# Another fixed order of two mixing stages, and another split of the weights' second parts between two engines

## The chip, the cores and the metric

The kernel runs on one core of one Trainium2 chip. The metric is the device time of one execution in microseconds (us), lower is better. The core's engines work side by side, each through its own instructions in the order in which they were issued, and they wait for one another through semaphores: TensorE (PE) for matmuls, VectorE (DVE), ScalarE (ACT), GpSimd (POOL), and SyncE (SP), which here only issues DMAs.

## The reference, cut to what matters

The input x is 512 x 1024 in float32. Two layers follow each other:

```python
h = rms_norm(x, norm_mix_g[l])
proj = h @ w_in[l]                       # 26 groups of 128 columns
o_att  = diff_attention(q, k, v, ...)    # 6 heads: softmax(q0 k0) - lam * softmax(q1 k1)
o_conv = short_conv(b, c, u, conv_w)     # y = b * causal 3-tap conv of c * u
o_rwkv = rwkv7_time_mix(...)             # 6 heads, a recurrence over the 512 positions
x = x + concat(o_att, o_conv, o_rwkv) @ w_out[l]
h = rms_norm(x, norm_mlp_g[l])
x = x + square(relu(h @ w_mlp_up[l])) @ w_mlp_down[l]
```

and at the end a last rms_norm. The part of a layer up to the product with w_out is called the mixing stage here, the rest its MLP stage.

## The kernel before, in words

**Layout.** Everything is kept transposed: x is eight tiles of 128 model channels by 512 positions. A product of 128 output columns is a chain of matmuls over eight channel tiles into one PSUM tile.

**Two-part products.** Each float32 operand is split into a rounded first part (hi) and the rest (lo), and a product takes three matmuls: hi by hi, hi by lo, lo by hi (`passes`, L550 to L559). The weights come in halves of four tiles, 256 KB a DMA, into three `raw` buffers. ACT rounds a half to `whi` (`casts`, L539). The second part `wlo` is raw - whi (`rests`, L548), and a letter of the string LO says for each half of a mixing stage whether DVE (x) or POOL (y) works it out. The first groups of layer 0 (HEAD) always go to DVE. `whi` and `wlo` have three buffers each.

**Order of the products.** PLAN gives, for each layer, the order in which the 26 column groups of w_in are multiplied. Groups 0 to 2, 3 to 5 and 6 to 8 are q, k and v of three pairs of attention heads; 9 to 14 the convolution's; 15 to 17, 18 to 20 and 21 to 23 r, k and v of the three pairs of recurrent heads; 24 and 25 the small inner products. After them come the eight column groups of w_out, in two halves of four channel tiles, and two groups of w_mlp_up. Loads, casts and second parts follow the same order (`halves_`).

**The steps.** A mixing stage is written as some twenty Python generators, each of which issues one instruction (or one group of small matmuls) at each step. Their letters: d loads (SP), w casts (ACT), x and y second parts (DVE, POOL), m the large matmuls (PE), e, q and n the entry and its norm, k constants, g decay rates, h the gate, R, S, T the three pairs of recurrent heads, r, s, t the block inverses that these need, A, B, C the three pairs of attention heads, U, V the convolution, o, p, i, N the output, its squares and the next norm. The two strings in ORDER, one for each layer, spell out in which order the steps are issued: `drive` (L157) reads "m3 R w" as three steps of m, one of R, one of w. Since every engine works through its instructions in the order of issue, this string fixes the order on each engine. Nothing reorders it later; only the waits for data and for free buffers come on top.

**The pieces that matter below.**

- Recurrent heads (`rwkv_pair`, L766): Gram products (pg), copied by ACT into nn; turned blocks; then products with the inverse (pzw, pap, pbs), then six steps of state (pst, L933, and L934 on DVE), then the outputs, a centring product (pc), a head norm and the gate. The head norm sums squares on PE (phs), takes an inverse square root in twelve small DVE operations (`rsqrt_steps`, L248), widens it on ACT (L739) and turns it back on PE (phb).
- Block inverse (`rwkv_inverse`, L985): POOL masks nn (nm, L990), DVE folds it (L992), it goes to DRAM and back in another layout (dn, nb); POOL then runs 30 small operations in 15 dependent pairs (tt L1004, xb L1006); the result goes through DRAM again (dm, xd); DVE spreads it (L1013, L1021) and turns it (yi, L1032); then PE and the copies alternate: px, py, pz, pzz.
- Attention (`att_pair`, L1096): q and k go through DRAM into stacked tiles; then for each of two heads and four query blocks two score products (sc), a masked maximum on DVE (L1163), two exponentials on ACT (L1168), small DVE operations (L1170, L1172), the difference of the two maps (L1174), transposes on PE (ptt) and a copy (L1183); at the end of a head the product with v (po).
- PSUM tiles come from three tags: mm (2 buffers, large products), at (2, attention), rp (4, everything else).

The MLP stages are issued by ordinary loops and have nothing to do with the strings.

Of the kernel before, what the change touches and what calls it, by code (L numbers as in the profile page):

```python
# [21 lines left out]
S = 512  # L22
# [3 lines left out]
C = 64  # L26
# [14 lines left out]
PLAN = ((24, 18, 15, 0, 3, 6, 25, 19, 21, 16, 1, 4, 22, 7, 20, 17, 2, 5, 11, 8, 13, 23, 9, 12, 14, 10),  # L41
        (24, 18, 15, 0, 3, 6, 19, 21, 25, 16, 1, 4, 7, 20, 22, 17, 11, 2, 13, 5, 9, 12, 8, 23, 14, 10))
# [7 lines left out]
LO = ("xxxxyxxxyxxxxxyyxyyxxyxyyxyxxxyxxyyyxyxyxyxxxxyyxxyxyyxyxxyyyxyxyxxxyxxx",  # L50
      "yyxxxxxxyyxxxyyyyyyxxxxyxyyyyyxxxyyyyyxxxyyyxyxxxyxyyyxyyxxxxyxyyxxxxyxy")

ORDER = (
# [1389 lines left out]
```

## Time and profile before

| | |
|---|---|
| median of three runs | 1301.89 us (1301.4 to 1303.5) |
| profiled execution, its own time | 1301.58 us |
| its span, first to last instruction | 1299.8 us |
| mean granted TensorE clock | 0.996 |
| mixing stage of layer 0 ("stage one") | 0 to 312.58 us |
| MLP stage of layer 0 ("stage two") | 312.58 to 648.42 us |
| mixing stage of layer 1 ("stage three") | 648.42 to 949.44 us |
| MLP stage of layer 1 and the last norm ("stage four") | 949.44 us to the end |

The bounds of the stages are read off the chain that ended last: it runs without a break from the second of the two early w_mlp_up groups on (312.58 and 949.44), and at 648.42 the products of w_in begin.

How to read the lines in the next section. The page's first part gives for each engine its busy time, its share of the span and its instructions; the second part gives busy tenths in 40 slices. A row of the table by stages has the stretch, its length, then busy time and count for PE, PEld (weight loads), DVE, ACT and POOL, then the granted clock, the share of the DMA engines and GB/s. A row of the waits says who waited for whom: us in total, times, the longest. A row of the groups has line, engine, operation, output and inputs with their shapes and count, then busy us and the mean ns of one, then the idle time before them and what ended it. A row of a tile's view has min/median/max in ns. A row of the timeline has start, length, line, engine, operation and count, and in brackets the idle time before it and what ended it.

### The profile page before, as it was taken

How to read it: one execution, taken by the hardware profiler on the slowest of the kernel's cores; microseconds unless marked ns; L12 is line 12 of the kernel's file. 1: busy time of each engine (PE TensorE's matmuls, PEld its weight loads, DVE VectorE, ACT ScalarE, POOL GpSimd, SP SyncE). 2: the span in 40 equal slices, each digit the busy share in tenths (PEclk: the TensorE clock that was granted, in tenths of full speed). 3: DMA queues.
4: the chain of work that ended last, by engine and by line, in shares of the span. 5: the costliest groups of instructions: out<-in, count | busy, mean ns of one | idle time of the engine just before them, and what ended most of it. 6: DMA issues, size and time to landing. Idle time of an engine off the chain costs nothing.

```text
span 1299.8 us, 25202 instructions
## 1 busy us (share of the span) xinstructions
PE 1270.7 (98%) x9531; PEld 1068.8 (82%) x9531; DVE 931.6 (72%) x1924; ACT 692.9 (53%) x1431; POOL 350.9 (27%) x440
## 2 busy tenths in 40 slices
PE   9999999999999999999999999999999999999997
PEld 6777777787889989889887777878778898898987
DVE  6777768967866938756557787877698497595754
ACT  6764655555644626436465756455567264363552
POOL 1362526233310201102317344451432021020010
PEclk9999999999999999999999999999999999999998
DMA  6523333132332332330235232331423323323121
GB/s 217 149 64 100 111 94 92 48 123 82 101 126 90 105 106 86 111 98 25 98 112 141 72 118 83 90 102 51 138 74 126 109 93 109 100 90 105 58 81 66
DMA packets 84425, 128.12 MB, mean 99 GB/s; under 512 B 21456, under 2 KB 24912, under 8 KB 84304
## 3 DMA queue, kind: packets, MB, share of 16 engines
q1 hardware_dynamic: 83584, 125.96, 30.9%
q8 instruction: 75, 1.23, 0.4%
q10 hardware_dynamic: 720, 0.55, 0.1%
q14 instruction: 46, 0.38, 0.1%
HBM read 117.30 MB, written 9.18 MB: 97 GB/s over the span
## 4 chain that ended last, share of the span: by engine, by line
PE 77%; DVE 10%; issue 2%; ACT 2%; DMA 1%; POOL 0%; POOLq 0%; SPq 0%; DVEq 0%; ACTq 0%
PE dn L180 23%; PE pj L180 14%; PE pp L180 11%; PE po L180 8%; PE up L180 8%; PE dnF L180 3%; DVE slo_p L1302 3%; DVE s L1307 2%; PE sc L180 1%; PE ptt L185 1%; PE pg L180 1%; DVE u L1324 1%; DVE c L1324 1%; PE pyy L180 1%; PE pst L180 0%
## 5 line engine op out<-in xcount | busy, mean ns | idle before, releaser
L1237 POOL TENSOR_TENSOR ml<-m,mh 128x512 fp32r<-128x512 f32 x64 | 101.6, 1587 | 504.4 <-ACT mh L1236 496.2
L231 ACT CAST whi<-raw 128x512 fp32r<-128x512 f32 x154 | 95.3, 621 | 201.6 <-PE dn L180 182.1
L232 DVE TENSOR_TENSOR wlo<-raw,whi 128x512 fp32r<-128x512 f32 x154 | 119.8, 778 | 85.8 <-ACT whi L231 85.6
L180 PE MATMUL dn<-ml,whi 128*128 128x512 f32 x448 | 174.4, 389 | 0.0
L180 PE MATMUL dn<-mh,whi 128*128 128x512 f32 x448 | 174.4, 389 | 0.0
L180 PE MATMUL dn<-mh,wlo 128*128 128x512 f32 x448 | 174.3, 389 | 0.0
L180 PE MATMUL pj<-ahim,whi 128*128 128x512 f32 x392 | 159.5, 407 | 0.0
L180 PE MATMUL pj<-alom,whi 128*128 128x512 f32 x392 | 159.4, 407 | 0.0
L180 PE MATMUL pj<-ahim,wlo 128*128 128x512 f32 x392 | 158.9, 405 | 0.0
L548 POOL TENSOR_TENSOR wlo<-raw,whi 128x512 fp32r<-128x512 f32 x64 | 87.7, 1371 | 197.4 <-ACT whi L539 165.3
L539 ACT CAST whi<-raw 128x512 fp32r<-128x512 f32 x138 | 85.3, 618 | 98.3 <-PE pj L180 42.5
L180 PE MATMUL pp<-thi,slo_p 128*128 128x256 f32 x352 | 100.1, 284 | 0.2
L180 PE MATMUL pp<-thi,shi_p 128*128 128x256 f32 x352 | 99.7, 283 | 0.5
L180 PE MATMUL pp<-tlo,shi_p 128*128 128x256 f32 x352 | 99.2, 282 | 0.0
L180 PEld LDWEIGHTS dn<-mh,wlo 128*128 128x128 f32 x448 | 84.1, 188 | 17.5
L180 PEld LDWEIGHTS dn<-mh,whi 128*128 128x128 f32 x448 | 84.1, 188 | 17.4
L180 PEld LDWEIGHTS dn<-ml,whi 128*128 128x128 f32 x448 | 84.1, 188 | 17.3
L1370 DVE TENSOR_TENSOR x<-dn,x 128x512 f32<-128x512 f32 x56 | 38.6, 690 | 75.7 <-PE dn L180 75.7
L180 PEld LDWEIGHTS pj<-ahim,whi 128*128 128x128 f32 x392 | 74.0, 189 | 15.1 <-issue 1.2
L180 PEld LDWEIGHTS pj<-ahim,wlo 128*128 128x128 f32 x392 | 74.0, 189 | 14.5 <-issue 1.0
L180 PEld LDWEIGHTS pj<-alom,whi 128*128 128x128 f32 x392 | 74.0, 189 | 14.4 <-issue 1.1
L180 PE MATMUL pp<-bhi,shi_p 128*128 128x256 f32 x264 | 74.7, 283 | 2.0 <-DVE u L1324 2.0
(399 smaller groups left out, 3244.5 us busy)
## 6 DMA issues: line engine op xcount, KB each, us to landing
raw<-wts SPq DMA_DIRECT2D x392, 256.0 KB, 2.7
qs<-dqhi SPq DMA_DIRECT2D x24, 128.0 KB, 3.8
ks<-dkhi SPq DMA_DIRECT2D x24, 128.0 KB, 4.0
x<-xT SPq DMA_DIRECT2D x8, 256.0 KB, 5.1
dqhi<-qhi SPq DMA_DIRECT2D x6, 256.0 KB, 3.4
dqlo<-qlo SPq DMA_DIRECT2D x6, 256.0 KB, 2.4
dkhi<-khi SPq DMA_DIRECT2D x6, 256.0 KB, 2.4
dklo<-klo SPq DMA_DIRECT2D x6, 256.0 KB, 2.8
```

Source lines behind the costliest of these rows:

```text
L180: ins = nc.tensor.matmul(*a, **k)
L185: ins = nc.tensor.transpose(*a, **k)
L231: act.copy(hi[:, :n], raw[:, :n])
L232: (pool if a and lean[0] else dve).tensor_tensor(lo[:, :n], raw[:, :n], hi[:, :n].bitcast(F32), ALU.subtract)
L539: yield act.copy(hi[:, :n], raw[:, :n])
L548: yield eng.tensor_tensor(lo[:, :n], raw[:, :n], hi[:, :n].bitcast(F32), ALU.subtract)
L1237: pool.tensor_tensor(lo, m, hi.bitcast(F32), ALU.subtract)
L1302: dve.tensor_tensor(lo, src, hi.bitcast(F32), ALU.subtract)
L1307: dve.tensor_tensor(t, a, b, op)
L1324: dve.tensor_tensor(out, pt, b, ALU.add)
L1370: dve.tensor_tensor(x[j], pt, x[j], ALU.add)
```

## The change

Only constants change: PLAN, LO and both strings of ORDER. No function is touched. The steps are the same in number and kind (2259 in layer 0, 2208 in layer 1). In layer 0, 33 of the 72 weight halves have their second part on POOL instead of 28, and 39 on DVE instead of 44 (six of them are HEAD's). In layer 1 it is 24 on POOL instead of 36, and 48 on DVE instead of 36.

The order strings are long. Below are PLAN, LO, and of ORDER the lines with the first steps and those in which the inverse of the first pair of layer 0 goes through px, py, pz, pzz (the r's) and on to pzw (an R), then those with the end of the second pair's head norm in layer 1 (S):

```diff
-PLAN = ((24, 18, 15, 0, 3, 6, 25, 19, 21, 16, 1, 4, 22, 7, 20, 17, 2, 5, 11, 8, 13, 23, 9, 12, 14, 10),
-        (24, 18, 15, 0, 3, 6, 19, 21, 25, 16, 1, 4, 7, 20, 22, 17, 11, 2, 13, 5, 9, 12, 8, 23, 14, 10))
+PLAN = ((24, 18, 15, 0, 3, 21, 6, 19, 25, 16, 22, 1, 4, 20, 7, 17, 2, 23, 5, 8, 11, 13, 9, 12, 14, 10),
+        (24, 18, 15, 0, 3, 21, 6, 25, 19, 16, 1, 4, 22, 7, 20, 17, 2, 5, 23, 11, 8, 13, 12, 9, 14, 10))
...
-LO = ("xxxxyxxxyxxxxxyyxyyxxyxyyxyxxxyxxyyyxyxyxyxxxxyyxxyxyyxyxxyyyxyxyxxxyxxx",
-      "yyxxxxxxyyxxxyyyyyyxxxxyxyyyyyxxxyyyyyxxxyyyxyxxxyxyyyxyyxxxxyxyyxxxxyxy")
+LO = ("yyxxxyxyxyxxyyyyxyxyxyyyxyxyxyxyxyxyxyxxxyxyxyyyxxxyxyxxxyyxxxyyyyxyxyxx",
+      "xxyxxxxyxxyyxxxxxxxxxxxyyyyxxxxyxxxxyyxyxxyyyxxxxxxyxxyyxxyyyxyyxyxxxxxx")
...
-         "d g d6 w x e d q m e w m x m w m2 d x m2 e m d m q e d m e d q d m q m d m e m e d m2 d q m q m d m e w m d m w m q d m d m x m d w m2 x d m d "
+         "g d7 w x e d q e m w m x w m x d m e m d m q d e m d e m d q2 m d e2 m d2 q m w d m q e d m x w m d m d m x m d w m2 d q m d m x e m d m2 d "
...
-         "A m r w S A d m S m r m r S x B m2 S d r A m S r m r m2 r m2 w m A m2 B2 m r y B2 A r2 m2 A d A m B r A2 r m r A m A m2 B2 R A w B A m A B "
+         "m h m2 r d m r w m r m S m3 r m y S m r m4 S A m d w A m2 S h m A r m y A2 m A2 m A m A m d S m S m2 r A m S w r2 m r2 m3 S A m h m x m r d "
+         "S2 m r S2 r A m S A m r S2 A r2 m A S A r w m A S m y A m r A m r2 d S m S2 r A m2 r m r m R S A3 m R2 m S m A m w B S A x B m R S d A B3 A "
...
-         "C m C S B T m C m S m S C m S m2 B T m S C m2 w B T m2 T S B y C S C T2 B d m T S m t T m2 S2 B t T S m B t S B S B m2 S m T B w S m T2 B x "
-         "t3 m T m2 T U d m U m2 S2 m T U T m S T m t U m T m T2 S w t U m T m5 S T m3 S t m T S m t y m S m2 w V m S T d m S m4 x m3 S d S t2 m S m t "
+         "m B2 S m B2 m3 S w S B x T d m T B S m S m2 S m S m2 T S m2 T m2 T w B S B S T2 B T S T t m B2 U S y t T B t S B T d B T2 B3 S m B T S m B S "
+         "m T t3 B S m T B S T B S B S B m S B T S m B S m T B S B m T S T B2 S B m2 S T t2 B t S t m B m t m T m w m2 t T m S2 T2 m S m3 T t m T m y "
```

105 rows, old and new, of the table ORDER are left out of this document.

## The prediction

> **What bounds the kernel now.** I read the page's first two parts, then the busy table over the four stages, then the waits of PE, then the timeline at the longest waits.
>
> ```profile
> PE 1270.7 (98%) x9531; PEld 1068.8 (82%) x9531; DVE 931.6 (72%) x1924; ACT 692.9 (53%) x1431; POOL 350.9 (27%) x440
> PE   9999999999999999999999999999999999999997
> ```
> ```profile
> 0.00:312.58 312.58, 301.65 (x2821) 237.32 (x2822) 234.40 (x593) 184.27 (x425) 114.36 (x181) 1.00 0.36 110
> 312.58:648.42 335.84, 334.44 (x1900) 293.76 (x1900) 235.48 (x366) 167.37 (x297) 60.24 (x40) 1.00 0.29 93
> 648.42:949.44 301.02, 294.46 (x2810) 235.89 (x2810) 221.37 (x559) 171.77 (x406) 122.41 (x183) 1.00 0.33 100
> 949.44:1299.80 350.36, 340.18 (x2004) 301.80 (x2002) 240.39 (x406) 169.51 (x304) 53.84 (x36) 0.99 0.29 93
> ```
>
> TensorE bounds it, at the full granted clock (1.00) through both mixing stages (rows one and three). The change reaches only these. PE stands still there for 312.58 - 301.65 = 10.9 us and 301.02 - 294.46 = 6.6 us. That 17.5 us is most of what an order can win; what it can lose has no such end. The other two stages keep their instructions and their times. The next view is what PE waited for, stage one and then stage three.
>
> ```profile
> PE px L180 <- DVE yi L1032: 2.3, 3, 1.0
> PE ptt L185 <- DVE pp L1174: 2.1, 4, 0.7
> ```
> ```profile
> PE phby L185 <- ACT rwy L739: 2.1, 2, 1.7
> PE ptt L185 <- DVE pp L1174: 1.2, 1, 1.2
> PE pst L180 <- DVE st L934: 0.7, 1, 0.7
> ```
>
> So PE waits at the ends of serial chains: the block inverse (px), the softmax (ptt), the head norm (phby), the state (pst). All 864 `m` letters of a stage are large matmuls that fill such chains. I therefore compare, old order with new, how much PE work stands between the two ends of a chain.
>
> **The change, part by part.** Both strings hold the same letters, 2259 and 2208 steps, and PE gets the same steps. Only their order moves, so nothing is saved on PE itself, and each term below is a wait. A large matmul counts 0.233 us, from this row of the chain of work (9.80/42):
>
> ```profile
> 656.05 9.80 PE pj L180 x42
> ```
>
> *1. The inverse chain.* From the first Gram product (pg) of a head pair to px run two copies, a mask, two DRAM round trips, 30 small POOL operations and a transposition. In stage one, pair 0:
>
> ```profile
> 58.76 0.35 ACT L831 COPY nn<-pg 128x256 f32<-128x256 f32 x1
> ```
> ```profile
> 68.39 0.21 POOL L1004 TENSOR_TENSOR tt<-nb,xb 64x15 f32<-64x15 f32 x1 [0.96 <-DMA nb<-dn]
> ```
> ```profile
> 85.17 0.21 POOL L1006 TENSOR_TENSOR xb<-xb,tt 64x15 f32<-64x15 f32 x1
> ```
> ```profile
> 95.51 0.59 PE L180 MATMUL px<-yi,ee 64*64 64x64 f32 x25 [0.96 <-DVE yi L1032]
> ```
>
> The chain took 36.7 us (58.76 to 95.51), 17.0 of them in POOL's small operations. PE, covering it, ran out 0.96 us early. Between pg and px the old order of stage one has 102, 105 and 109 large matmuls for pairs 0, 1 and 2; the new one has 103, 78 and 154. The smaller PE groups beside them, each counted from its first matmul to the next group's (pzz below: 171.35 to 171.98), go from 9.7, 9.7 and 7.3 us to 5.6, 8.4 and 10.4. With 0.233 us a large matmul, cover goes from 33.5, 34.2 and 32.7 us to 29.6, 26.6 and 46.3. Pair 2 gains cover; pair 0 loses 3.9 us and pair 1 loses 7.6. POOL's own load inside the 30 operations moves too: pair 0 gets three weight halves where it had one, pair 1 two where it had three.
>
> ```profile
> L548 DVE TENSOR_TENSOR wlo<-raw,whi x74: 671/683/1627, 24.1 to 938.6; 128x512 fp32r<-128x512 f32 x74
> L548 POOL TENSOR_TENSOR wlo<-raw,whi x64: 1263/1290/1811, 22.9 to 943.3; 128x512 fp32r<-128x512 f32 x64
> ```
> ```profile
> L548 POOL TENSOR_TENSOR wlo<-raw,whi 128x512 fp32r<-128x512 f32 x28 | 38.3, 1367 | 87.6 <-ACT whi L539 66.3 <-DVE st L934 13.1 <-PE po L180 6.0
> ```
>
> That is +2.6 us for pair 0; pair 1 loses 1.29 and one more POOL operation of that size, -2.6. Upper end: the chain keeps its length but for POOL's load, and PE's other waits beside it stay (36.7 - 0.96 - 33.5 = 2.2 us; I use it for both). Pair 0 then waits 36.7 + 2.6 - 29.6 - 2.2 = 7.5 us, pair 1, whose chain I take as long, 36.7 - 2.6 - 26.6 - 2.2 = 5.3 us; less the 2.3 us that go, +10.5 us. Lower end: the chain shrinks with its cover. The last row speaks for some of this: 66.3 us of POOL's idle time before a weight half ended with ACT's whi, so POOL is paced by the weights' turn in the order. Then all px waits vanish, -2.3 us. I take the middle, **+4 us**. In stage three the counts are 104, 100, 114 and 108, 102, 106: no change.
>
> *2. The short links after px.* px, pz and pzz each feed the next PE step through two ACT copies:
>
> ```profile
> 171.35 0.69 PE L180 MATMUL pzz<-x,rt 32*32 32x32 f32 x32
> 171.98 0.44 PE L180 MATMUL sc<-ks,qs 96*128 96x128 f32 x2
> ...
> 173.56 0.34 PE L180 MATMUL pzw<-ab,x 64*64 64x128 f32 x4
> ```
> ```profile
> 172.09 0.75 ACT L1070 COPY x<-pzz 32x256 f32<-32x256 f32 x2 [0.47 <-PE pzz L180]
> ```
>
> The copies end at 172.84, 0.86 us after pzz gave PE free (171.98); with the hand-over some 0.95 us. The old stage one covers all nine links with 1.16 us or more, this one with 1.6. The new one covers px to py with 3 matmuls, 1 and a 0.46 us group, and 3; pzz to pzw with 4, with one 0.8 us group, and 3; one pz link has 0.86. Those below 0.95 lack 0.26, 0.26, 0.26, 0.09, 0.02, 0.15 and 0.25 us, in sum 1.3. The state links run from one pst through DVE to the next:
>
> ```profile
> L180 PE MATMUL pst<-st,ad x60: 217/273/324, 114.1 to 896.8; 128*128 128x64 f32 x60
> L934 DVE SCALAR_TENSOR_TENSOR st<-pst,dc,db x36: 272/280/285, 113.6 to 897.6; 128x64 f32<-128x64 f32 x36
> ```
>
> The need is 0.273 + 0.280 and the hand-overs, some 0.6 us. Five of these 15 links have two matmuls or fewer between (0.47 us) in the new order, none in the old: 0.7 us more. Upper end 2.0, lower end 0 if PE is late anyway: **+1.5 us**. Stage three's balance over the same links is under 0.5 us: nothing.
>
> *3. Softmax links.* From the second score product to the transposes:
>
> ```profile
> L1168 ACT ACTIVATE pp<-pp,mx 128x128 f32<-128x128 f32 (+3 forms) x48 | 26.6, 555 | 13.8 <-DVE mx L1163 13.0 <-DVE rst L263 0.6
> L1163 DVE CUSTOM_DVE_ANT_0 pp<-sc,caus 128x128 f32<-128x128 f32 (+3 forms) x48 | 22.1, 486 | 9.0 <-PE sc L180 8.8
> L1174 DVE SCALAR_TENSOR_TENSOR pp<-pp,sm,pp 128x128 f32<-128x128 f32 (+3 forms) x24 | 15.7, 656 | 0.5
> L1168 ACT ACTIVATION_READ_ACCUMULATOR pp<-pp,mx 128x1 f32 x48 | 9.0, 186 | 0.0
> L1172 DVE SCALAR_TENSOR_TENSOR sm<-s0q,nlam,sm 128x1 f32<-128x1 f32 x24 | 6.4, 268 | 0.4
> L1170 DVE RECIPROCAL sm<-sm 128x1 f32<-128x1 f32 x24 | 3.9, 161 | 13.0 <-ACT pp L1168 12.8
> ```
>
> The need is 0.486 + 0.555 + 0.186 + 0.161 + 0.268 + 0.656 = 2.3 us and queueing. With under 3.3 us of cover stand 9 of 24 links in the old stage one and 12 in the new; 11 and 7 in stage three. At the waits quoted (2.1/9 and 1.2/11 us a link) this is +0.7 - 0.4 = **+0.3 us**; a full softmax need uncovered would be 2.3.
>
> *4. The engine choice.* Stage one takes 5 halves from DVE to POOL (POOL 28 to 33), stage three 12 from POOL to DVE (36 to 24). On DVE those are 12 x 0.683 = 8.2 us more, beside 301.02 - 221.37 = 79.7 us of its idle time; without that cover they would cost the 8.2. What POOL's operations do to DVE is seen here:
>
> ```profile
> 843.34 2.68 DVE L263 SCALAR_TENSOR_TENSOR rst<-rst,rsx 128x8 f32<-128x8 f32 x1
> ```
> ```profile
> 843.48 1.29 POOL L548 TENSOR_TENSOR wlo<-raw,whi 128x512 fp32r<-128x512 f32 x1
> 844.74 1.25 POOL L869 TENSOR_TENSOR pd_2lo<-pd,pd_2hi 128x512 fp32r<-128x512 f32 x1
> ```
> ```profile
> L263 DVE SCALAR_TENSOR_TENSOR rst<-rst,rsx x72: 147/166/2681, 22.0 to 1291.7; 128x8 f32<-128x8 f32 x54, 128x4 f32<-128x4 f32 x12, 128x2 f32<-128x2 f32 x6
> ```
>
> An operation of 0.166 us took 2.68, to the end of two POOL operations, and stage three's 1.7 us wait at phby follows it. Fewer POOL halves in stage three make such hits rarer, but in the new order that same link (second pair, phsy to phby) has 10 matmuls and three transposes where it had 31 and five groups. Two inverse square roots lie interleaved in it, 22 operations of 0.166 us, so its own length, 22 x 0.166 + 0.68 + 0.62 = 5.0 us, meets about 3.4 us of cover. A wait of 1.6 stands where one of 1.7 stood. For the rest -0.5 us, between -2.1 (the other quoted waits of stage three, 1.2 + 0.7, and this 0.2) and +2.3.
>
> The Trainium skill ("SBUF — State Buffer", "Who interferes with whom") says that a VectorE instruction with two SBUF inputs and a GpSimd instruction that reads SBUF exclude each other for a whole instruction; the 2.68 us row agrees. By that rule the 12 halves taken off POOL in stage three free up to 12 x 1.29 = 15.5 us of such locks; the first rival below is this case.
>
> *5. The rest.* The products' order moves the value product of a pair by one group and some DMA issues with it; each raw load still goes out on SP three buffers ahead, in the products' order, and the stacked q and k loads keep their place behind them on that queue. The ends of both stages, from the last output products on, are the same but for single letters. Nothing, between -0.5 and +1.
>
> **Sum.** 4 + 1.5 + 0.3 - 0.5 = +5.3 us on the profiled execution's 1301.58 us, which lies 0.3 us under the median of 1301.89: about **1307 us**.
>
> **The rivals.**
>
> *Faster.* The waits are collisions of DVE with POOL, not short cover. For it: the 2.68 us row, and the lighter POOL in stage three. Against it: stage one gets more POOL halves, and its counted cover shrinks. If POOL's pacing lets the inverse chain shrink (-2.3), the short links cost nothing, and stage three loses its quoted waits at ptt and pst (1.2 + 0.7) with 0.2 at phby, it is -4.4: 1297 us. It decides from where the px chain of pair 1 in stage one runs in under 29 us.
>
> *No change.* The chain shrinks half way and the wins of stage three meet it: +1, 1302.5 us.
>
> *Much slower.* The chain keeps its length: 10.5 + 2.0 + 0.7 us, and no gain in stage three: +13.2, 1315 us. For it: POOL's part was 17.0 us though its 30 operations are small.
>
> **How the numbers follow.** Forecast (1303.5 to 1311) 0.48; much slower 0.20; no change 0.14; faster 0.18. This measurement tells about 0.2% (2.6 us) from no change. Slower 0.48 + 0.20 = 0.68, same 0.14, faster 0.18. The range from 1298 to 1316 leaves out part of the fastest and of the slowest case.
>
> **What would show it.** Stage one longer by 3 to 8 us, most of it as waits of px on yi for pairs 0 and 1 and none for pair 2; stage three within 1.5 us; a phby wait near its middle; DVE busy up in stage three, POOL down by about 15 us. Wrong, if px of pairs 0 and 1 waits under 1 us each: then the chain follows its cover. Also wrong, if stage three moves by over 3 us: then the engine choice is worth more than I gave it.

## The result, and the profile after

The changed kernel takes **1308.03 us** (median of five runs, 1306.51 to 1310.77), the kernel before 1302.44 us beside it (five runs, 1301.4 to 1304.77). The ratio is 1.0045 with a 95% interval of 1.0034 to 1.0055: it is slower by 5.6 us. The profiled execution of after took 1308.03 us itself, 6.45 us more than that of before, so its stages can be set against those of before.

The table by stages of after, with the bounds read off its chain in the same way (columns: stretch, its length, then busy time and count of PE, PEld, DVE, ACT and POOL, the granted clock, DMA share, GB/s):

```profile
0.00:320.76 320.76, 306.54 (x2823) 237.36 (x2824) 228.43 (x588) 184.74 (x426) 116.47 (x186) 1.00 0.34 107
320.76:656.75 335.99, 334.39 (x1899) 293.26 (x1898) 237.28 (x368) 166.75 (x296) 57.53 (x38) 1.00 0.28 93
656.75:955.42 298.67, 295.65 (x2811) 235.91 (x2811) 217.11 (x569) 173.78 (x406) 105.61 (x173) 1.00 0.33 101
955.42:1306.20 350.78, 340.07 (x2003) 301.04 (x2001) 241.58 (x406) 169.67 (x304) 52.98 (x36) 0.99 0.28 92
```

Stage one is longer by 320.76 - 312.58 = **8.2 us**, stage three shorter by 301.02 - 298.67 = **2.35 us**; the stages that kept their code moved by 0.15 and 0.42 us. In stage one PE stands still for 320.76 - 306.54 = 14.2 us (10.9 before), and is booked as busy for 4.9 us more with the same work. The second part is waiting too: a large matmul is booked with 0.39 us, but the next one starts after 0.233 us if nothing holds it, so each break of the stream hides up to 0.16 us in "busy".

What PE waited for in stage one of after (columns: who for whom, us in total, times, the longest):

```profile
PE ptt L184 <- DVE pp L1173: 2.3, 5, 0.8
PE px L179 <- DVE sm L1169: 2.1, 1, 2.1
PE pssm L179 <- DVE accm L335: 1.6, 1, 1.6
...
PE pj L179 <- DVE pk L660: 0.9, 1, 0.9
PE pj L179 <- DVE vf L1130: 0.9, 1, 0.9
PE sc L179 <- ACT pT L1182: 0.8, 3, 0.4
PE prbm L179 <- issue: 0.8, 1, 0.8
PE phby L184 <- ACT rwy L738: 0.8, 1, 0.8
```

px waits once, for 2.1 us, where it waited three times and 2.3 us before (the profile names sm, the DVE operation right behind yi). The new waits are others: pssm, the product of the first norm at the entry, 1.6 us; and large products (pj) that wait for an eviction, twice 0.9 us. In stage three of after the same view has the phby waits (2.1 us) and that of the state (0.7 us) gone:

```profile
PE ptt L184 <- DVE pp L1173: 1.0, 2, 0.6
PE pv L184 <- DVE zv L665: 0.8, 1, 0.8
PE prbf L179 <- DVE rrf L263: 0.6, 1, 0.6
```

To count the hidden part too, I took for every matmul the time to the next one's start, less the time under which the fastest fifth of its shape stay in stage one of before (0.23 us for a large one), and summed it by what the next matmul writes. "Short links" are all PE steps from py to the end of the state, pbv among them. In us, for before, after and two kernels of the experiments below:

| stage one | before | after | s1_order | s1_engines |
|---|---|---|---|---|
| px | 4.2 | 3.5 | 1.5 | 3.0 |
| short links after px, state | 15.3 | 17.8 | 17.8 | 16.3 |
| softmax (sc, ptt) | 10.2 | 12.5 | 13.4 | 10.1 |
| head norms (phs, phb) | 3.8 | 3.1 | 2.6 | 6.3 |
| entry (pssm, prbm, pw) | 2.2 | 4.4 | 3.8 | 2.0 |
| large products (pj, po) | 21.0 | 22.1 | 24.3 | 21.6 |
| Gram products and all others | 15.5 | 16.5 | 17.3 | 15.9 |
| sum | 72.2 | 79.9 | 80.6 | 75.2 |

| stage three | before | s3_order | s3_engines | s3_all |
|---|---|---|---|---|
| px | 1.2 | 1.9 | 1.2 | 1.2 |
| short links, state | 17.2 | 16.4 | 16.7 | 16.1 |
| softmax | 8.6 | 8.7 | 10.4 | 8.4 |
| head norms | 4.5 | 2.4 | 2.6 | 2.4 |
| entry | 0.5 | 0.5 | 0.9 | 0.9 |
| large products | 19.5 | 18.8 | 19.6 | 18.7 |
| Gram products and all others | 16.1 | 19.1 | 15.7 | 17.5 |
| sum | 67.6 | 67.8 | 67.1 | 65.3 |

So the 8 us of stage one are no single wait. They lie in the short links (+2.5), the softmax (+2.3), the entry (+2.2), large products and others (+2.1); px and the head norms fell (0.7 each). One caution: in the profiled execution of s1_order 3.4 us of stage one (22.10 to 25.51) ran at half the granted clock, which puts up to some 2 us into its column; before, after and s1_engines have no such stretch in stage one (the last section).

**My theory after the result** was that the order takes cover from many chains at once, and that px, the largest term of the forecast, was not one of them. The rival was collisions: POOL's operations hold DVE's, and the engine choice decides.

### The profile page after: what moved, and what is told of

Its sections match the earlier page's. It is cut to its first block, busy times and chain, and to the rows that moved or that the text cites. A ratio compares the mean times of both kernels' runs of the same rounds, so it can differ in the third digit from the quotient of the medians.

```text
span 1306.2 us, 25237 instructions
## 1 busy us (share of the span) xinstructions
PE 1276.6 (98%) x9531; PEld 1067.6 (82%) x9531; DVE 924.4 (71%) x1931; ACT 694.9 (53%) x1431; POOL 332.6 (25%) x433
## 4 chain that ended last, share of the span: by engine, by line
PE 80%; DVE 11%; issue 3%; ACT 2%; DMA 2%; POOL 1%; SPq 0%; POOLq 0%; DVEq 0%; ACTq 0%
PE dn L179 23%; PE pj L179 18%; PE pp L179 10%; PE po L179 8%; PE up L179 7%; PE dnF L179 3%; DVE slo_p L1301 3%; DVE s L1306 2%; PE sc L179 1%; PE ptt L184 1%; DMA raw<-wts 1%; DVE c L1323 1%; PE pg L179 1%; DVE u L1323 1%; PE pst L179 1%
## 5 line engine op out<-in xcount | busy, mean ns | idle before, releaser
L547 POOL TENSOR_TENSOR wlo<-raw,whi 128x512 fp32r<-128x512 f32 x57 | 74.9, 1314 | 210.7 <-ACT whi L538 181.1
L179 PEld LDWEIGHTS dn<-ml,whi 128*128 128x128 f32 x448 | 84.1, 188 | 17.2
L179 PEld LDWEIGHTS pj<-ahim,whi 128*128 128x128 f32 x392 | 74.1, 189 | 17.3 <-DVE pk L660 1.4
```

Source lines behind the costliest of these rows:

```text
L179: ins = nc.tensor.matmul(*a, **k)
L547: yield eng.tensor_tensor(lo[:, :n], raw[:, :n], hi[:, :n].bitcast(F32), ALU.subtract)
```

## The experiments

All leave nothing of the computation out. Times are ratios to the kernel before, run beside each on the same chip, with 95% intervals. For lengths of stages I use two marks of each trace: A, from the start to PE's first product with w_mlp_down in layer 0 (360.52 us in before), and B, from the first pj of layer 1 to the same product there (349.18). Where a stage was left as in before, A was 360.52, 360.64, 362.13, 362.42 and 362.60, and B 349.02 to 349.72. So one profile tells 2 us in stage one and 0.7 us in stage three. The last section shows where the 2 us come from: the granted clock. A of after (368.82) is free of it.

### Each stage alone

```diff
 s1_all: PLAN[0], LO[0], ORDER[0] of after; PLAN[1], LO[1], ORDER[1] of before
 s3_all: PLAN[0], LO[0], ORDER[0] of before; PLAN[1], LO[1], ORDER[1] of after
```

> PLAN, LO and order string of layer 0 from after, layer 1 as before: stage one alone is changed. In the one profile of after, stage one is 320.76 us against 312.58 (+8.2), stage three 298.67 against 301.02 (-2.35). If the two stages are independent, this kernel is 8 us over before (about 1310), its stage three 301 us as in before. If part of the 8.2 us is chance of one execution, it is +4 to +6 and another profile shows other waits. In the forecast's terms (+4 for px, +1.5 short links, +0.3 softmax) it would be +5.8.

> PLAN, LO and order string of layer 1 from after, layer 0 as before: stage three alone is changed. If the stages are independent, 2.3 us under before (about 1300). The forecast's terms for this stage (order 0, engine choice -0.5) say within 0.5 us of before.

Measured: s1_all 1.0076 (1.0064 to 1.0089), 9.9 us slower; A 370.56, B 349.72. s3_all 0.9979 (0.9969 to 0.9988), 2.7 us faster; A 362.60, B 346.91, as in after (346.68). The stages are independent, and both effects come again: stage one +8 (A 368.82 in after and 370.56 here, against a mean of 361.7) and stage three -2.6. The waits come again too, within 0.2 us (s1_all: px 2.2 us once, pssm 1.4, pj twice 0.9), so they belong to stage one's new order and engines, not to one execution. The forecast's -0.5 at most for stage three is refuted.

### Order and engine choice of stage three

The order of after with each half on the engine that it had before, and the other way round:

```diff
 s3_order, LO[1] on after's PLAN[1] and ORDER[1]:
-xxyxxxxyxxyyxxxxxxxxxxxyyyyxxxxyxxxxyyxyxxyyyxxxxxxyxxyyxxyyyxyyxyxxxxxx
+yyxxxxxxyyyyxxyyxyyxxxxyyyxyyyxxyyxxxxxyxyyyyyxyxyxyyyxyyxxxxyxyyxxxxyxy
 s3_engines, LO[1] on before's PLAN[1] and ORDER[1]:
-yyxxxxxxyyxxxyyyyyyxxxxyxyyyyyxxxyyyyyxxxyyyxyxxxyxyyyxyyxxxxyxyyxxxxyxy
+xxyxxxxyxxxxxxyyxxxxxxxyyxxxyyxyxyxxyyxxxxyxxxyyxxxyxxyyxxyyyxyyxyxxxxxx
```

> Layer 1 has after's order of products and steps, but each half of the weights keeps the engine that it had before (36 on POOL, 36 on DVE): a letter x or y is changed in its place. If the gain of stage three comes from 12 halves fewer on POOL (fewer DVE operations stretched beside POOL's), this shows none of it: 0 to +2 us against before. If it comes from the order (the head norm's and softmax links have other cover), this shows all of it, -2 us.

> Layer 1 has before's order of products and steps, but each half has the engine that after gives it (24 on POOL, 48 on DVE): a letter x or y is changed in its place. If the gain of stage three comes from fewer collisions, this has it: -2 us or more, with the 1.7 us wait of phby gone. If it comes from the order, 0; if DVE as the longer queue delays the chain ends, +1 to +2.

Measured: s3_order 1.0010 (1.0001 to 1.0019), B 349.46; s3_engines 0.9993 (0.9984 to 1.0002), B 348.61. Neither has the gain (s3_engines has 0.9 us, with none inside its interval), and both together have 2.7 us: the expectation of one cause fails. The table of stage three shows why. Each of the two takes the head norm's waits away (4.5 to 2.4 and 2.6), and each pays it back elsewhere: the order with the old engines in Gram and other products (+3.0, among them 0.6 us of pot), the engines with the old order in the softmax (+1.8; ptt waits 2.8 us). Together the softmax stays at 8.4. An order and the engines beside it are one choice.

The stretch of DVE says the same. Summing, over DVE's operations that ran over 0.3 us above the fast tenth of their form beside a POOL operation, what they ran over: 20.8 us in stage three of before (22 operations), 11.5 in s3_order (12, with the same 36 halves on POOL), 16.3 in s3_engines (19), 10.1 in s3_all (11). So which operations meet counts for more than how many halves POOL has. Nor does this sum give the time: s3_order halves it and gains nothing.

### One letter

```diff
 LO[1]:
-yyxxxxxxyyxxxyyyyyyxxxxyxyyyyyxxxyyyyyxxxyyyxyxxxyxyyyxyyxxxxyxyyxxxxyxy
+yyxxxxxxyyxxxyyyyyyxxxxyxyyyyyxxxyyyyyxxxyyyxxxxxyxyyyxyyxxxxyxyyxxxxyxy
 ORDER[1]:
-S T m3 S t m T S m t y m S m2 w V m S
+S T m3 S t m T S m t x m S m2 w V m S
```

> Before, with one single weight half of stage three (group 8, second half; the one on POOL at 843.48) moved from POOL to DVE. There an operation of 0.166 us on DVE took 2.68 us, to the end of this half and of the next POOL operation, and PE waited 1.7 us at phby behind it. If POOL's operation holds DVE's, this one letter takes away 1.3 us or more of that wait and the kernel is 1 to 2 us faster; if the DVE operation waited for something else, the phby wait stays and nothing is gained.

Measured: 0.9983 (0.9974 to 0.9991), **2.2 us faster**, B 347.43. The timeline of this kernel at the place where an operation took 2.68 us before:

```profile
843.65 0.20 DVE L263 SCALAR_TENSOR_TENSOR rst<-rst,rsx 128x8 f32<-128x8 f32 x1
...
843.88 0.17 DVE L264 SCALAR_TENSOR_TENSOR ry<-rst,ry 128x8 f32<-128x8 f32 x1
843.99 0.69 DVE L548 TENSOR_TENSOR wlo<-raw,whi 128x512 fp32r<-128x512 f32 x1
```

The operation takes 0.20 us again, the half runs on DVE for 0.69 us behind the chain, and of the phby waits (2.1 us) this is left:

```profile
PE phby L185 <- ACT rwy L739: 0.4, 1, 0.4
```

POOL's operation held DVE's, and one letter is worth nearly as much as the whole change of stage three (2.2 and 2.7 us, with intervals that overlap). The rule of the Trainium skill named in the prediction ("SBUF — State Buffer", "Who interferes with whom") says this of a DVE operation with two SBUF inputs; the run agrees with 0.20 us for 2.68.

### Order and engine choice of stage one

```diff
 s1_order, LO[0] on after's PLAN[0] and ORDER[0]:
-yyxxxyxyxyxxyyyyxyxyxyyyxyxyxyxyxyxyxyxxxyxyxyyyxxxyxyxxxyyxxxyyyyxyxyxx
+xxxxxxxxyxxyxxyyxxyxyxxyxyxxyxyxxyxxyyxyxyxyxxyyxxyxyyxyxxyyyxyxyxxxyxxx
 s1_engines, LO[0] on before's PLAN[0] and ORDER[0]:
-xxxxyxxxyxxxxxyyxyyxxyxyyxyxxxyxxyyyxyxyxyxxxxyyxxyxyyxyxxyyyxyxyxxxyxxx
+xxxxxxxyxyyyxyyyxxxyyyxyxyxyxyxyxyxyxyxxxyxyxyyyxxxyxyxxxyyxxxyyyyxyxyxx
```

> Layer 0 has after's order of products and steps, but each weight half keeps the engine of before (28 on POOL instead of 33); layer 1 as before. Forecast: the loss comes from cover that the order takes away, so nearly all of it stays: +7 to +9 us against before in stage one. Rival (collisions, or POOL's halves between the 30 small operations): 5 halves fewer on POOL give back 3 us or more.

> Layer 0 has before's order, but each weight half has the engine that after gives it (33 on POOL); layer 1 as before. Forecast: within 1.5 us of before. Rival (collisions): +2 us or more. In stage three the two parts of the change did not add (order +1.3, engines -0.9, both -2.7); if an order and its engines belong together, both of these kernels are slower than before by more than the forecast allows.

Measured: s1_order 1.0053 (1.0040 to 1.0066), +6.9 us, A 369.51; s1_engines 1.0024 (1.0016 to 1.0033), **+3.1 us**, A 363.76. Here the parts add up (0.53 + 0.24 against 0.76% for s1_all). The order is the larger part, as forecast, and it costs 6.9 us although px does not wait once in s1_order (1.5 in the table, 4.2 before): the forecast's largest term is not where the order loses. The engine choice costs 3 us where the forecast had 0 for stage one. With before's order its loss lies in the head norms (3.8 to 6.3 in the table). The timeline of s1_engines in the second pair's head norm:

```profile
225.87 1.58 POOL L548 TENSOR_TENSOR wlo<-raw,whi 128x512 fp32r<-128x512 f32 x1 [1.22 <-ACT whi L539]
226.23 1.25 DVE L263 SCALAR_TENSOR_TENSOR rst<-rst,rsx 128x8 f32<-128x8 f32 x1
...
227.41 1.26 POOL L1030 TENSOR_TENSOR ee<-nn,cst 128x512 f32<-128x512 f32 x1
227.51 1.19 DVE L264 SCALAR_TENSOR_TENSOR ry<-rst,ry 128x8 f32<-128x8 f32 x1
...
228.74 0.62 ACT L739 COPY rwy<-ry 128x512 f32<-128x512 f32 x1 [2.94 <-DVE ry L264]
```

Two operations of 0.166 us run to the ends of two POOL operations, and PE waits behind them:

```profile
PE phby L185 <- ACT rwy L739: 1.6, 1, 1.6
```

It looks like the collision of stage three once more, made by a half (group 10's second) that the new LO moves from DVE to POOL; no run moves this half back alone. In before only the operation ee met this chain, and PE waited 0.7 us.

After itself does not pay this: with the new order its head norms fell (3.8 to 3.1), and DVE's stretch, summed as above, is 14.9 us in stage one of after, 19.8 in before, 17.9 in s1_order and 25.7 in s1_engines. What the engine choice costs beside the new order (3 us from s1_order to s1_all) is not located, and part of it may be the clock: the mean granted clock is 0.994 in all five runs of s1_all, and 0.995 to 0.997 in those compared of s1_order; the table has 2.0 more at px in after than in s1_order.

### Cover of the inverse chain

In before, for each pair of stage one, 10 large matmuls are put from ahead of px to behind it (px_early10), or 5 from behind to ahead (px_late5); the first pair as an example:

```diff
 px_early10:
-S r m r m A2 r2 m w A m A m2 A m y A m2 B A m r w S
+S r2 A2 r2 w A3 y A B A r m10 w S
 px_late5:
-A m r w S A d m S m r m r S x B m2 S d
+A m6 r w S A d S r2 S x B S d
```

> Before, with the last 10 large matmuls ahead of px put directly behind it, for each of the three pairs of stage one: 2.33 us less cover for each inverse chain, all else in its order. If a chain has a length of its own, as the forecast's upper end took it, px waits 2.3 us longer in each pair: +7 us. If the chain follows its cover (POOL and DVE come to its steps earlier when PE stands), it is under +3.5 us, and the chain from nn to px is shorter by 1 us or more a pair. The forecast's middle lies between, +4.5.

> Before, with the next 5 large matmuls behind px put ahead of it, for each of the three pairs of stage one: 1.17 us more cover for each chain. If a large matmul of cover is worth 0.233 us wherever PE waits, the three px waits (2.3 us) go and the kernel is 2 us faster. If the wait only moves (to py and pz, which lose 5 matmuls of cover and have the two copies between them), it is 0 to +2.

Measured: px_early10 1.0066 (1.0054 to 1.0078), **+8.6 us**; px_late5 0.9989 (0.9981 to 0.9998), -1.4 us. The waits of px in px_early10:

```profile
PE px L180 <- DVE yi L1032: 5.8, 2, 3.2
PE px L180 <- DVE sm L1172: 2.8, 1, 2.8
```

That is 8.6 us for 2.3 in before: 6.3 us for 30 matmuls, 0.21 us each. The chains from nn to px are 36.6, 37.4 and 36.0 us, as long as in before (36.7, 37.3, 36.1). So a chain does **not** follow its cover when only PE's work is moved: the price of the forecast, 0.233 us a matmul, nearly holds. The measured +8.6 is over the +7 for a reason of the hardware, told last. px_late5 takes the three px waits away and gives part of it back: the sum of the head norms rises by 0.9 us (phbk waits 2.0 for 1.2), the short links by 0.8.

Then why did pair 0 wait 2.1 us in after where the forecast's upper end had 7.5, and pair 1 not at all where it had 5.3? From nn to px it took 35.0 and 33.1 us (58.09 to 93.07, 119.81 to 152.90). The rows of the second, from nn to POOL's first operation, the one half that runs among the 30, yi and px:

```profile
119.81 0.37 ACT L830 COPY nn<-pg 128x256 f32<-128x256 f32 x1 [0.79 <-PE pg L179]
```
```profile
129.21 0.21 POOL L1003 TENSOR_TENSOR tt<-nb,xb 64x15 f32<-64x15 f32 x1
```
```profile
138.78 1.29 POOL L547 TENSOR_TENSOR wlo<-raw,whi 128x512 fp32r<-128x512 f32 x1
```
```profile
151.36 0.71 DVE L1031 STREAM_TRANSPOSE yi<-x 128x512 f32<-128x512 f32 x1
```
```profile
152.90 0.29 PE L179 MATMUL px<-yi,ee 64*64 64x64 f32 x4
```

POOL's part, from 129.21 to 142.2, took 13.0 us, where it took 17.7 in before. In both kernels the 30 operations alone take some 12 us (11.6 to 12.2) with their hand-overs. The rest is what the order puts among them: in before 5.4 us of other operations (three halves, a pd_lo) for pair 1, in after 1.4 (one half); for pair 0, 2.8 and a wait of 2.1 ahead of the half in before (1.5 of it until ACT had cast the half's whi, at 76.71), 4.1 and no wait in after. For pair 2 it turned round (8.2 us of others and 3.0 us of waits ahead of them: 22.8 us), but that pair had cover. For pair 1 this is the smaller part. Its yi ended at 152.07, 32.3 us after nn began, 1.8 less than the forecast's 36.7 - 2.6; and PE came to px 0.8 us later still: PE itself took 33.1 us where the forecast counted 26.6 of work and 2.2 of other waits. The waits of PE in this stretch are 2.0 us at pj and 1.5 at ptt, so time that the forecast put at px was spent ahead of it.

### Two gaps, and the entry

s1_gaps is s1_all with PE work put into two gaps, s1_entry is s1_all with before's first 175 steps:

```diff
 s1_gaps, ORDER[0]:
-s S s A m s m R2 s A2 m s m R w s2 T A s2 R A S m s m s m2 s
+s2 A m s m R s A2 m s m T S R2 w s2 A s2 R A S m s m s m2 s
...
-w m x m3 s d m s m2 s m s m y m3 w B s d s m s m T m3 s m s m A m s m s A m2 x m w A d S m A2 m y A2
+w m x m3 A2 s d m s m2 s m s m y m3 w B A4 s d s m s m T m3 s m s m2 s m s m2 x m w d S m2 y A
 s1_entry, ORDER[0], its beginning:
-g d7 w x e d q e m w m x w m x d m e m d m q d e m d e m d q2 m d e2 m d2
+d g d6 w x e d q m e w m x m w m2 d x m2 e m d m q e d m e d q d m q m d e
```

> As s1_all (after's stage one), with PE steps that were ready anyway put into two gaps in the cover of the second pair's inverse: the tri-product pa and the gate product pgt behind the end of product group 20, with its eviction pk ahead of them, and one transposition and two score products of attention behind the end of group 7. In s1_all PE waits 0.9 us at each of these two places for an eviction, since the other PSUM buffer of the large products is still held by group 22. If these waits are losses of their own, stage one is 1.8 us shorter than in s1_all. If the second pair's inverse chain has its length (33.1 us, px waiting 0), they stand in the place of a px wait: px then waits about 1 us and the gain is 0.8 us or less.

> As s1_all, with the first 175 steps in before's order (up to the first norm's last product prbm; 58 large matmuls stand ahead of pssm instead of 50, and 72 ahead of prbm instead of 61), and after's order for all the rest. If the norm's chain at the entry is what PE waits for there (pssm 1.4 to 1.6 us in after, prbm 0.8), the wait of pssm goes and stage one is 1 to 2 us shorter than in s1_all. If the entry is bound by the first loads, or the loss comes back at the next wait, it is 0.

Measured: s1_gaps 1.0062 (1.0049 to 1.0075), A 367.83; s1_entry 1.0061 (1.0048 to 1.0075), A 369.60; s1_all had 1.0076 (1.0064 to 1.0089), A 370.56. Both point to a gain, but the intervals overlap. In A, s1_gaps is 1.0 us under after and s1_entry 0.8 over it, each with one stretch at half clock that after does not have: the size stays open. The mechanism can be seen. In the waits of s1_gaps no pj waits for pk or vf any more, and px waits once only, for pair 0:

```profile
PE ptt L185 <- DVE pp L1174: 2.7, 4, 1.3
PE px L180 <- DVE sm L1170: 1.6, 1, 1.6
PE pssm L180 <- DVE accm L336: 1.4, 1, 1.4
PE sc L180 <- ACT pT L1183: 1.4, 4, 0.6
```

The px of pair 1 did not take the wait over: from nn to px it took 32.1 us (33.1 in after, and 34.6 in the profile of s1_all, which has 3.4 us at half clock there). So these two waits were losses of their own, though ptt takes 0.4 us more than in after. By the program they come from PSUM: in the new order the v products of the recurrent pairs (groups 21, 22, 23) stand early and their evictions (pv) late. Group 22's stands 114 large matmuls behind its end (86 in before), group 21's 49 (1) and group 23's 48 (10). So long, one of the two buffers of the large products is held, and each next group must wait for the eviction of the one before it. In before the order has other PE steps at such borders; in after, at groups 20 and 7, none.

In the waits of s1_entry pssm is gone, and these stand close behind it (pw has 0.7 in after and s1_all, pj for ahim 0.2 in s1_all):

```profile
PE pw L180 <- DVE pr L661: 1.0, 1, 1.0
...
PE prbm L180 <- issue: 0.6, 1, 0.6
PE pj L180 <- ACT ahim L320: 0.5, 1, 0.5
```

58 large matmuls ahead of pssm cover its chain, 50 do not; but part of the wait comes back.

### The parts that gained

```diff
 best_parts: ORDER[0] of px_late5, PLAN[0] and LO[0] of before; PLAN[1], LO[1], ORDER[1] of after
```

> Stage one of px_late5 (before's, with 5 large matmuls put ahead of each px) and stage three of after: the parts that gained. If the stages add, -1.4 (px_late5) and -2.6 (s3_all): about 4 us under before, under both kernels. If not, -2.6.

Measured: 0.9975 (0.9965 to 0.9984), 1299.91 us beside 1303.14: 3.2 us under before, A 361.06, B 346.59. The sum expected was about 4. It beats both kernels; most of it is stage three, and since the intervals of this kernel and s3_all overlap, a gain by px_late5's part is not shown here.

## Why the prediction was right, point by point

The forecast was 1307 us, and 1308.03 was measured; the sign and the size came out, and "stage one longer by 3 to 8 us" nearly (8.2). "Stage three within 1.5 us" did not (-2.35). Its reasons came out only in part, and errors of both signs nearly cancelled: that the number is so close is luck.

- **1, the inverse chain (+4): mis-sized, it was about -0.5** (waits of px, both rows of the view, 2.5 to 2.1 us, in the table 4.2 to 3.5). px_early10 nearly confirms the price of a matmul of cover. What failed is, for pair 0, "the chain keeps its length but for POOL's load": 36.7 + 2.6 = 39.3 us by the forecast, 35.0 measured. That load was counted as three and two halves for pairs 0 and 1, and the traces have two and one; the "17.0 of them in POOL's small operations" held 2.8 us of other operations and 2.1 of waiting, and the order moved some of that away. For pair 1 it is, more than that, "PE's other waits beside it stay": 2.2 us by the forecast, 6.5 measured (33.1 - 26.6). "Wrong, if px of pairs 0 and 1 waits under 1 us each" was met for pair 1 (0), not for pair 0 (2.1).
- **2, the short links (+1.5): right in the main**, +2.5 in the table, 0.8 of it at pbv, which the forecast did not count. The state's links have 0.6 of it, as forecast (0.7); py, which was to lose by px's copies, has nothing.
- **3, softmax links (+0.3): too small**, +2.3. The links were counted alone, not what else stands in DVE's queue ahead of pp; that this is the reason is not shown, since no run took this part by itself.
- **4, the engine choice (-0.5): the step that failed most.** It cost 3 us in stage one (s1_engines, and s1_all against s1_order), and in stage three the order had no gain without it. I had the 2.68 us row, but spread it over the stage instead of asking, chain by chain, which POOL operation lies beside it. POOL did fall by 16.8 us in stage three (15 forecast). DVE did not rise: 8.2 us of halves were added, and the stretch counted above fell from 20.8 us to 10.0. "A wait of 1.6 stands where one of 1.7 stood" did not come either. The first and the last operation of that inverse square root in after's timeline:

```profile
838.25 0.16 DVE L255 TENSOR_SCALAR rsx<-phsy 128x8 f32<-128x8 f32 x1
...
840.56 0.16 DVE L263 SCALAR_TENSOR_TENSOR ry<-rst,ry 128x8 f32<-128x8 f32 x1
```

The two interleaved chains took 2.5 us where I took 22 x 0.166 = 3.65: the starts lie closer than the durations, and nothing was stretched.

- **5, the rest (0, at most +1): too small.** The entry (+2.2), and the large products and others (+2.1), with the held PSUM buffers, were not looked for.
- **The rivals.** "Collisions" was put as the case in which the kernel gets faster. The mechanism was right where it was tested (one letter, 2.2 us in stage three), but it is not what made stage one slower: the larger part there comes with the order alone (s1_order, +6.9 us), while DVE is stretched less than before.

What stays open: the softmax part of stage one, where the engine choice loses beside the new order, and how much of the 8.2 us the entry and the PSUM gaps are, since profiles of this stage differ by 2 us with the clock.

## What to carry to other kernels

A chain's cover can be counted in matmuls, but its length is set by what the order queues among its steps on the other engines: walk those queues too. Look first at chains of many tiny VectorE operations: one large GpSimd operation beside them stretched 0.17 us to 2.68, and moving that one away was worth nearly as much as a new order and engine choice for a whole stage. With two PSUM buffers, a product that ends early and is evicted late leaves one buffer for all others. Before two profiles are compared to the microsecond, compare their granted clocks.

## What the runs showed of the hardware

Waits of PE can cost more than themselves, because the granted clock may fall behind them. In px_early10, around the first pair's px (PE's timeline):

```profile
96.00 1.13 PE L180 MATMUL px<-yi,ee 64*64 64x64 f32 x32 [2.54 <-DVE yi L1032]
...
98.51 0.63 PE L180 MATMUL pj<-ahim,whi 128*128 128x512 f32 x1
98.94 0.63 PE L180 MATMUL pj<-alom,whi 128*128 128x512 f32 x1
99.36 0.63 PE L180 MATMUL pj<-ahim,wlo 128*128 128x512 f32 x1
```

Large matmuls start 0.43 us apart instead of 0.233, and are booked with 0.63 instead of 0.39. The table by stretches of the same kernel has the granted clock (the number behind POOL's) at half:

```profile
93.00:96.00 3.00, 0.45 (x1) 0.21 (x2) 2.96 (x4) 0.48 (x1) 2.87 (x3) 0.88 0.06 12
96.00:99.00 3.00, 3.00 (x37) 2.50 (x38) 1.56 (x6) 1.31 (x4) 0.24 (x1) 0.50 0.23 75
99.00:102.00 3.00, 3.00 (x9) 2.32 (x8) 0.47 (x1) 1.12 (x3) 0.00 (x0) 0.50 0.00 0
102.00:105.00 3.00, 3.00 (x45) 2.31 (x44) 1.89 (x6) 1.08 (x4) 1.00 (x1) 0.99 0.45 163
```

It came at all three px waits (2.54, 2.8 and 3.2 us). In the table's terms the large products cost 25.7 us here, 21.0 in before: 4.7 us for three waits.

Shorter waits can do it too, and not in every execution. Stage one of s3_all is that of before, instruction by instruction, with the same waits of PE (px 1.0 us, up to 96.04 in s3_all, and phbk 1.2 us, up to 98.84). The same stretch in s3_all and in before:

```profile
98.58:101.99 3.41, 3.15 (x39) 2.39 (x40) 1.37 (x4) 1.25 (x4) 1.11 (x1) 0.50 0.45 151
```
```profile
98.58:101.99 3.41, 3.41 (x47) 2.62 (x46) 2.75 (x6) 1.23 (x3) 1.29 (x1) 1.00 0.43 156
```

Such stretches at half clock, of 3.41 us each, lie in the mixing stages of nine of the fourteen profiles, all in stage one (two in s1_all, and 6.83, 3.41 and 3.41 us in px_early10): s1_all, s1_order and s1_gaps have one some 2 us behind the end of the pssm wait of 1.1 to 1.4 us at the entry, while after, with 1.6 us there, has none. They explain why A scatters: with before's stage one and no such stretch it is 360.52 and 360.64, with one 362.13, 362.42 and 362.60, so a stretch cost 1.5 to 2.1 us. After has none in stage one, so its +8.2 us are not the clock's. The Trainium skill ("TensorE: Matmul & The Clock Gate", "HAM oscillation — how this bites in real kernels") has the clock halved by idle gaps over some 3.4 us; the halving agrees, while here gaps of 1 to 2.5 us were enough in some executions.
